# Attention outputs of a hybrid attention and gated-MLP layer: uncut fp32 probabilities and values, two branches on two halves of the array's columns

## The chip, the cores and the metric

One Trainium2 chip, one core. The metric is the device time of one execution in microseconds (us), median over runs. The kernel before takes 1041.9 us (three runs, 1041.83 to 1042.65).

## The reference, cut to what matters

One layer is computed for 1024 prompt tokens and for 8 sample tokens with cached keys. Only the prompt's attention is touched by the change. It has three branches: over compressed blocks (`o_c`), over chosen blocks (`o_s`) and over a window of 512 keys (`o_w`). Eight heads of 64 dimensions share two groups of keys and values, four heads to a group.

```python
def nsa_core(q, qpos, kc, vc, ks, vs, kw, vw, kwpos):
    ...
    s_s = jnp.einsum('bqgrd,bgqnld->bqgrnl', qg, k_sel).astype(jnp.float32) * scale
    ...
    p_s = jax.nn.softmax(s_s, axis=-1).reshape(B, Tq, N_KV, GQA, n_sel, L_SLC)
    o_s = jnp.einsum('bqgrnl,bgqnld->bqgrd', p_s.astype(dt), v_sel)
    ...
    s_w = jnp.einsum('bqgrd,bkgd->bqgrk', qg, kw).astype(jnp.float32) * scale
    p_w = jax.nn.softmax(jnp.where(m_w, s_w, NEG), axis=-1)
    o_w = jnp.einsum('bqgrk,bkgd->bqgrd', p_w.astype(dt), vw)
```

Around it stand the input projections (modulated RMS norm, then `w_in`), the rotary parts, a gated spatial MLP, a gated merge of the two branches' projections and the output projection. All inputs and outputs are fp32.

## The kernel before, in words

Most matrix products are made from halves: an fp32 value x is cut into hi (rounded to fp32r, the type of a one-pass matmul) and lo = x - hi, and a product takes three one-pass matmuls, hi by hi, hi by lo and lo by hi. Channel-major projections (`ct_proj`, line 883; tiles `mm`, weights `c0h`, `c0l`, `c1h`, `c1l`, inputs `hh`, `hl`) do that 128 channels by 344 tokens at a time. They run as "jobs" (`stream`, line 900), which fill TensorE beside decode and attention.

The order of the work on every engine is fixed when the program is built. Each piece of work is a generator that yields what it waits for. `Plan.go` (line 237) always runs a step of the stream that would wait least by the plan's own estimate of the time (`Plan.cost`, line 165, has a cost for each instruction), and the instructions go to the engines in that order. All engine calls go through a helper, so the profile shows line 217 for each of them, and tiles tell them apart. `paced` (line 871) holds the jobs back so that they last as long as the attention.

The prompt's attention works on 16 tiles (`TILES`): a group g of heads and 128 queries i. For a tile, `front` prepares the queries and the maxima. `scores` (line 1704) then walks over its spans (`spans`, line 1574): a span is a branch w (1 window, 0 chosen blocks) and 128 keys. Two fp32r matmuls give the scores of 128 keys by 512 (four heads by 128 queries) in a bank `st`, ScalarE's exponential writes `pt`, and on the diagonal GpSimd masks it. There are 132 spans in all: 60 of the window and 72 of the chosen blocks.

`low` (line 1728) cuts `pt` into halves `p`: the hi half by ScalarE or VectorE (`HI_DVE`), the lo half by VectorE or GpSimd (`ON_POOL`). `outputs` (line 1743) adds a span to the branch's bank `pv` with three one-pass matmuls. The values `vv` of a branch are kept as [v hi | 64 columns of ones | v lo], so that the first and third matmul also give the sums of p in rows 64 to 127 of the bank:

```python
pe.matmul(x, lhsT=v[:, 0:128], rhs=p2[:, 0], start=first, stop=False, skip_group_check=True)
pe.matmul(x[0:64], lhsT=v[:, 128:192], rhs=p2[:, 0], start=False, stop=False, skip_group_check=True)
pe.matmul(x, lhsT=v[:, 0:128], rhs=p2[:, 1], start=False, stop=False, skip_group_check=True)
```

`weigh` (line 1773) copies a branch's output (`u`) and its row of sums (`sr`) out of the bank, and `close` (line 1793) divides, weighs by gates and adds the branches. A matmul's place in the array follows from its operands: its weights' columns lie where the output's rows begin. In the kernel before every output begins at row 0 of its bank.

Of the kernel before, what the change touches and what calls it, by code (L numbers as in the profile page):

```python
# [24 lines left out]
EPS = 1e-6  # L25
# [3 lines left out]
class Pack:  # L29
    """Constants that depend on the shapes alone, as columns of one [128, n] array."""  # L30
# [62 lines left out]
class Plan:  # L93
    """Estimates when the engines get to what has been emitted, so that independent streams of work can be
    emitted in an order in which the engines wait little. It has no part in what is computed."""
# [35 lines left out]
    def meet(x, y):  # L131
        """Whether two accesses to a tile, as box() gives them, overlap."""
# [8 lines left out]
    def after(self, ap, writes_only, engine=None):  # L141
        """When the accesses to the elements of ap are over."""
# [22 lines left out]
    def cost(self, engine, name, outs, ins, size, start):  # L165
        if engine == "pe":
# [4 lines left out]
            elif dt == F32:  # L171
                cost, passes = max(4 * n / 2.4, 208 * m / 128), 4
# [87 lines left out]
def nsa_gmlp_step(ctx: ExitStack, tc: tile.TileContext, a: dict):  # L260
# [29 lines left out]
    def free_bank(tag):  # L290
        """Goes on when a bank can be written, as far as other streams let it."""
# [15 lines left out]
    def rows(name, n, m=128):  # L307
        """The n elements of an input on each of m partitions."""
# [38 lines left out]
    def rsqrt(out, x, scale, n, p=128):  # L347
        """out = (x * scale + EPS) ** -0.5"""
# [24 lines left out]
    def weights(todo):  # L373
        """Loads slices (key, source, columns) in order and cuts them into hi and lo, but for those used as they are."""
# [46 lines left out]
    def x_turned(first):  # L421
        """RMS-normalised x, transposed: every other tile."""
# [26 lines left out]
    def x_loads():  # L449
        """The tiles of x behind the weights of the modulation, which all wait for."""  # L450
# [38 lines left out]
    def modulation():  # L489
        """Shift and scale of the samples and the prompt (column 8), and from them h."""  # L490
# [1532 lines left out]
```

## Time and profile before

| | |
|---|---|
| median of 3 runs | 1041.9 us (1041.83 to 1042.65) |
| span of the profiled execution | 1039.6 us |
| TensorE (PE) busy | 1018.3 us, 98% of the span |
| weight loads (PEld) busy | 878.7 us, 85% |
| VectorE (DVE) busy | 657.1 us, 63% |
| ScalarE (ACT) busy | 468.5 us, 45% |
| GpSimd (POOL) busy | 305.5 us, 29% |

The profiled execution shows its span, from its first instruction to its last; no other time of it is given, and the median of the runs is 2.3 us above it. The page lists for each engine how long it was busy, in 40 slices how busy it was and which clock TensorE was granted, and for groups of instructions their number, time and what they waited for. In the name of a group `pv<-p,vv` the tile written stands left of the arrow and the tiles read stand right of it. The end of a matmul is modelled in the profile, so a matmul's cost in a stream is read from the distance of two starts in the timeline.

### The profile page before, as it was taken

To read this page: it belongs to the slowest core of one execution; us is meant where nothing else is said; L and a number is where in the kernel's file an instruction comes from. 1 tells how busy PE (TensorE), PEld (TensorE's weight loads), DVE (VectorE), ACT (ScalarE), POOL (GpSimd) and SP (SyncE) were. 2 spreads that over 40 slices of the span, in tenths; PEclk is the share of its full clock that TensorE was granted. 3 is DMA by queue.
4 is the path that set the end of the run, shared out by engine and by line. 5 is a ranking of instruction groups with operands and counts; after the bars stand their busy time and mean duration, and the time that the engine had idled before them with its cause. 6 is when DMAs were issued, how large, how long until landed. Compare 5 with 4: busy or idle time off the path is not lost. (4 is left out here: it accounts for less than half of the span.)

```text
span 1039.6 us, 16376 instructions
## 1 busy us (share of the span) xinstructions
PE 1018.3 (98%) x5747; PEld 878.7 (85%) x5747; DVE 657.1 (63%) x1372; ACT 468.5 (45%) x984; POOL 305.5 (29%) x332
## 2 busy tenths in 40 slices
PE   7999999999999999999999999999999999999998
PEld 2589977879999999987878788778788999998776
DVE  5676786354668766578787868895753147675322
ACT  5763332001332244767766677677666242232000
POOL 0453565454221110013334332433333100251000
PEclk9999999999999999999999999999999999999999
DMA  9735451103875745521212121211111478554321
GB/s 328 263 95 175 135 185 52 61 22 129 277 213 149 256 152 192 151 67 41 79 53 72 35 64 49 68 38 51 50 58 59 126 248 254 187 163 146 120 91 62
DMA packets 106311, 130.33 MB, mean 125 GB/s; under 512 B 27299, under 2 KB 71525, under 8 KB 106230
## 3 DMA queue, kind: packets, MB, share of 16 engines
q1 hardware_dynamic: 101622, 112.52, 33.7%
q0 software_dynamic: 4608, 16.78, 5.2%
q8 instruction: 45, 0.74, 0.3%
q14 instruction: 36, 0.29, 0.1%
HBM read 98.95 MB, written 30.23 MB: 124 GB/s over the span
## 5 line engine op out<-in xcount | busy, mean ns | idle before, releaser
L217 PE MATMUL pv<-p,vv 128*128 128x512 f32 (+1 forms) x396 | 111.7, 399 | 0.5 <-DVE p L217 0.4
L217 PE MATMUL mm<-hh,c0h 128*128 128x344 f32 x320 | 105.3, 329 | 0.0
L217 ACT ACTIVATE pt<-st 128x512 f32<-128x512 f32 x132 | 78.7, 596 | 58.5 <-PE st L217 56.1
L217 PE MATMUL mm<-hh,c1h 128*128 128x344 f32 x320 | 104.9, 328 | 0.0
L217 PE MATMUL mm<-hl,c0h 128*128 128x344 f32 x320 | 102.3, 320 | 0.0
L217 PE MATMUL mm<-hl,c1h 128*128 128x344 f32 x320 | 102.2, 319 | 0.0
L217 PE MATMUL mm<-hh,c1l 128*128 128x344 f32 x320 | 102.2, 319 | 0.0
L217 PE MATMUL mm<-hh,c0l 128*128 128x344 f32 x320 | 102.2, 319 | 0.0
L217 PE MATMUL st<-R,L 128*128 128x512 f32 (+1 forms) x264 | 88.2, 415 | 0.0
L217 PEld LDWEIGHTS pv<-p,vv 128*128 128x128 f32 (+1 forms) x396 | 65.7, 172 | 22.4 <-DVE p L217 1.9
L217 DVE TENSOR_TENSOR p<-pt,p 128x512 fp32r<-128x512 f32 x88 | 69.4, 794 | 17.7 <-ACT p L217 17.1
L217 POOL TENSOR_TENSOR p<-pt,p 128x512 fp32r<-128x512 f32 x44 | 60.0, 1364 | 53.9 <-ACT p L217 53.9
L217 ACT ACTIVATE p<-pt 128x512 fp32r<-128x512 f32 x94 | 59.1, 629 | 13.6 <-POOL pt L217 12.3
L217 POOL TENSOR_SCALAR_AFFINE_SELECT pt<-pt 128x512 f32<-128x512 f32 x40 | 29.3, 732 | 121.7 <-ACT pt L217 119.8
L217 PE MATMUL mx<-L,R 128*128 128x512 f32 (+3 forms) x204 | 61.7, 364 | 1.8 <-DVE bm L217 1.1
L217 PEld LDWEIGHTS mm<-hh,c1h 128*128 128x128 f32 x320 | 60.3, 188 | 2.9 <-issue 0.2
L217 PEld LDWEIGHTS mm<-hh,c0h 128*128 128x128 f32 x320 | 60.4, 189 | 2.5 <-issue 0.2
L217 PEld LDWEIGHTS mm<-hh,c1l 128*128 128x128 f32 x320 | 60.3, 188 | 2.5
L217 PEld LDWEIGHTS mm<-hh,c0l 128*128 128x128 f32 x320 | 60.3, 188 | 2.1
L217 PEld LDWEIGHTS mm<-hl,c0h 128*128 128x128 f32 x320 | 60.1, 188 | 0.0
L217 PEld LDWEIGHTS mm<-hl,c1h 128*128 128x128 f32 x320 | 60.1, 188 | 0.0
L217 ACT ACTIVATE th<-mm 128x344 f32<-128x344 f32 x68 | 30.9, 454 | 58.3 <-PE mm L217 58.0
(497 smaller groups left out, 2669.3 us busy)
## 6 DMA issues: line engine op xcount, KB each, us to landing
t_db<-th SPq DMA_DIRECT2D x24, 172.0 KB
t_da<-th SPq DMA_DIRECT2D x24, 172.0 KB
th<-t_db SPq DMA_DIRECT2D x24, 172.0 KB
th<-t_da SPq DMA_DIRECT2D x24, 172.0 KB
graw<-in_w_ada_dram SPq DMA_DIRECT2D x16, 256.0 KB
araw<-in_w_ada_dram SPq DMA_DIRECT2D x16, 256.0 KB
xt<-in_x_dram SPq DMA_DIRECT2D x8, 512.0 KB
eraw<-in_w_ada_dram SPq DMA_DIRECT2D x16, 256.0 KB
```

What stands on the lines that cost most here:

```text
L217: r = getattr(real, name)(*args, **kw)
```

## The change

The probabilities `pt` are not cut any more, nor are the values: `vv` is fp32 with 64 columns, `low` goes, and its two or three elementwise instructions of a span with it. A span has one fp32 matmul with 64 columns. The window's output goes to rows 64 to 127 of a bank and that of the chosen blocks to rows 0 to 63 of the same bank, so the two lie on different halves of the array's columns. `spans` now alternates between the branches as long as both have keys, and `outputs` emits four spans in a row.

The sums of p have no matmul of their own in a span: `total` adds the `pt` of a branch up elementwise into `acc` (VectorE, every third span GpSimd), and at the end of a tile two fp32 matmuls with 32 columns of ones, at rows 0 and 32 of a bank `mx`, sum `acc` over the keys. `weigh` reads both sums in one copy. `pt` has 8 buffers in place of 4. In `Plan.cost` an fp32 matmul with at most 64 columns counts half. The changed file has no docstrings and section comments; that part of the diff is left out here.

```diff
@@ Plan.cost
             elif dt == F32:
-                cost, passes = max(4 * n / 2.4, 208 * m / 128), 4
+                cost, passes = max(4 * n / 2.4 / (2 if m <= 64 else 1), 208 * m / 128), 4
@@ attention of the prompt
-    L1, L2, vv = ({(g, w): areg.tile(shape, FR, name=f"{n}{g}{w}") for g, w in ((0, 0), (0, 1), (1, 0))}
-                  for n, shape in (("L1", [128, T]), ("L2", [96, T]), ("vv", [128, 8, 192])))
+    L1, L2, vv = ({(g, w): areg.tile(shape, dt, name=f"{n}{g}{w}") for g, w in ((0, 0), (0, 1), (1, 0))}
+                  for n, shape, dt in (("L1", [128, T], FR), ("L2", [96, T], FR), ("vv", [128, 8, 64], F32)))
...
-    PT_BUFS, P_BUFS = 4, 4
+    PT_BUFS = 8
...
-    one = areg.tile([128, 64], F32, name="one")
+    one = areg.tile([128, 32], F32, name="one")
@@ keys
-                v = v8[:, 4 * hf:4 * hf + 4]
-                split(v[:, :, 0:64], v[:, :, 128:192], v4)
-                act.activation(v[:, :, 64:128], one[:, None, :].to_broadcast([128, 4, 64]), AF.Copy)
+                act.activation(v8[:, 4 * hf:4 * hf + 4], v4, AF.Copy)
@@ spans
-        return [(1, k) for k in range(max(0, i - 4), i + 1)] + [(0, k) for k in range(i + 1)]
+        window, chosen = [(1, k) for k in range(max(0, i - 4), i + 1)], [(0, k) for k in range(i + 1)]
+        return [x for two in zip(window, chosen) for x in two] + chosen[len(window):]
@@ scores
-                plan.add(low(g, i, n, pt), 0)
+                plan.add(total(g, i, n, w, pt), 0)
@@ low, total
-        yield lambda: flying[0] < P_BUFS
-        flying[0] += 1
-        p2 = areg.tile([128, 2, 512], FR, name="p2", bufs=P_BUFS)
-        if n % 3 in HI_DVE:
-            dve.tensor_copy(p2[:, 0], pt)
+        key = g, i, w
+        if key not in sums:
+            sums[key] = pt
         else:
-            act.activation(p2[:, 0], pt, AF.Copy)
-        yield p2[:, 0]
-        (pool if n % 3 in ON_POOL else dve).tensor_tensor(p2[:, 1], pt, p2[:, 0].bitcast(F32), op=OP.subtract)
-        waiting[0] -= 1
-        cut[g, i, n] = p2
+            old = sums[key]
+            if key not in added:
+                added.add(key)
+                sums[key] = areg.tile([128, 512], F32, name="acc", bufs=4)
+            (pool if n % 3 in ON_POOL else dve).tensor_tensor(sums[key], old, pt, op=OP.add)
+        cut[g, i, n] = pt
@@ outputs
-            o, x, todo = {}, None, spans(i)
-            for n, (w, k) in enumerate(todo):
-                yield lambda: (g, i, n) in cut and (g, w, "v") in built
-                p2 = cut.pop((g, i, n))
...
-                yield p2[:, 1]
-                v = vv[g, w][:, k, :]
-                pe.matmul(x, lhsT=v[:, 0:128], rhs=p2[:, 0], start=first, stop=False, skip_group_check=True)
-                pe.matmul(x[0:64], lhsT=v[:, 128:192], rhs=p2[:, 0], start=False, stop=False, skip_group_check=True)
-                pe.matmul(x, lhsT=v[:, 0:128], rhs=p2[:, 1], start=False, stop=False, skip_group_check=True)
...
+            todo = spans(i)
+            yield lambda: open_[0] < 2
+            open_[0] += 1
+            x = bank("pv")
+            for n0 in range(0, len(todo), 4):
+                four = range(n0, min(n0 + 4, len(todo)))
+                yield lambda: all((g, i, n) in cut for n in four) and (g, 0, "v") in built and (g, 1, "v") in built
+                pts = [cut.pop((g, i, n)) for n in four]
+                yield pts[-1]
+                for n, pt in zip(four, pts):
+                    w, k = todo[n]
+                    pe.matmul(x[64 * w:64 * w + 64], lhsT=vv[g, w][:, k, :], rhs=pt, start=n < 2, stop=False, skip_group_check=True)
+                    spanned[0] += 1
+                if four[-1] + 1 == len(todo):
+                    yield sums[g, i, 0]
+                    yield from free_bank("mx")
+                    b = bank("mx")
+                    for w in range(2):
+                        pe.matmul(b[32 * w:32 * w + 32], lhsT=one, rhs=sums.pop((g, i, w)), start=True, stop=True)
+                waiting[0] -= len(four)
                 yield 0
@@ weigh
-        act.activation(sr[64:65], x[64:65], AF.Copy)
-        if j not in s8s:
-            s8s[j] = areg.tile([128, 8], F32, name="s8", bufs=U_TILES)
-        dma(s8s[j][64 * w:64 * w + 64], sr[64:65])
+        act.activation(sr, b[0:33], AF.Copy)
+        s8s[j] = areg.tile([128, 8], F32, name="s8", bufs=U_TILES)
+        for w in range(2):
+            dma(s8s[j][64 * w:64 * w + 64], sr[32 * w:32 * w + 1])
```

TensorE's order around the outputs of two spans, before (`vv_4490` holds the values of the chosen blocks, `vv_4491` those of the window, `mm` is a job's projection, `st` the scores, `mx` the maxima):

```order
L217 MATMUL mm<-hl,c1h 128x344
L217 MATMUL st<-R,L_4485 128x512
L217 MATMUL st<-R_6627,L_4488 128x512
L217 MATMUL pv<-p_7314,vv_4491 128x512
L217 MATMUL pv<-p_7314,vv_4491 64x512
L217 MATMUL pv<-p_7314,vv_4491 128x512
L217 MATMUL mx<-kc_4495,R 128x64 x4
```

And in the changed program, where the outputs of four spans stand in a row:

```order
L217 MATMUL st<-R,L_4485 128x512
L217 MATMUL st<-R_4753,L_4488 128x512
L217 MATMUL pv<-pt,vv_4491 64x512
L217 MATMUL pv<-pt,vv_4490 64x512
L217 MATMUL pv<-pt,vv_4491 64x512
L217 MATMUL pv<-pt,vv_4490 64x512
L217 MATMUL mx<-L_4484,R 128x512
```

Three matmuls of a span became one of 64 rows, and the branches alternate. Counted over the whole program, the 164 new matmuls (132 of spans, 32 of sums) stand in 51 uninterrupted runs: 24 of four spans that alternate (window, chosen, window, chosen), 5 of one span of each branch, 14 of two sums alone, and 8 of other kinds, among them the 12 spans of the chosen blocks that have no partner in the window.

The sums of a tile on TensorE, in the changed program, between the maxima of the next tiles:

```order
L217 MATMUL mx<-L_4485,R 128x384
L217 LDWEIGHTS ident_bf
L217 MATMUL mx<-far_bf,ident_bf 128x128
L217 MATMUL mx<-acc,one 32x512 x2
L217 MATMUL mx<-L_4485,R 128x256
L217 LDWEIGHTS ident_bf
L217 MATMUL mx<-tri_bf,ident_bf 128x128
```

Both matmuls are new, 32 in the 16 tiles; the program before has nothing in their place.

TensorE's order at the start, during the modulation (`gh`, `gl`, `araw`: weights of the modulation, `xt`: rows of x that are transposed), as the difference of the two programs:

```order
 L217 MATMUL mm<-gl,cs 42x512
 L217 MATMUL mm<-araw,cT 9x512
+L217 MATMUL mx<-main,xt 128x128 x8
 L217 MATMUL mm<-gh,cs 42x512
 L217 MATMUL mm<-gl,cs 42x512
@@ -29,5 +30,4 @@
 L217 MATMUL mm<-gl,cs 42x512
 L217 MATMUL mm<-araw,cT 9x512
-L217 MATMUL mx<-main,xt 128x128 x8
 L217 MATMUL mm<-gh,cs 42x512
 L217 MATMUL mm<-gl,cs 42x512
```

Eight transposes stand a few matmuls earlier. The fp32 matmuls `mm<-araw,cT` of 9 columns are untouched, but the plan's estimate for them is halved, and the order moves in many such places up to the decode.

## Rows read from the trace of the kernel before

**Rows 1.** The page: busy time by engine; TensorE and its granted clock in 40 slices.

```profile
PE 1018.3 (98%) x5747; PEld 878.7 (85%) x5747; DVE 657.1 (63%) x1372; ACT 468.5 (45%) x984; POOL 305.5 (29%) x332
...
PE   7999999999999999999999999999999999999998
...
PEclk9999999999999999999999999999999999999999
```

**Rows 2.** Busy time by stretch: length, engines with counts, granted clock, DMA, GB/s.

```profile
0.00:36.00 36.00, 29.55 (x99) 8.85 (x100) 19.04 (x38) 19.55 (x34) 2.81 (x9) 1.00 0.95 341
36.00:150.00 114.00, 111.78 (x614) 98.85 (x613) 88.20 (x219) 57.57 (x131) 61.54 (x69) 1.00 0.48 150
150.00:260.00 110.00, 108.35 (x546) 89.25 (x544) 56.17 (x116) 14.12 (x26) 56.33 (x50) 1.00 0.22 74
455.00:805.00 350.00, 344.97 (x1945) 286.84 (x1945) 254.89 (x560) 243.65 (x516) 125.77 (x140) 1.00 0.18 55
```

**Rows 3.** Waits of TensorE from 400 to 810 us: total us, times, longest.

```profile
PE mx L217 <- DVE bm L217: 1.7, 4, 0.8
PE mx L217 <- DVE BT L217: 1.6, 2, 1.0
...
PE pv L217 <- DVE p L217: 0.4, 1, 0.4
```

**Rows 4.** TensorE's timeline around two spans: start us, length, instruction, count.

```profile
705.24 0.85 PE L217 MATMUL pv<-p,vv 128*128 128x512 f32 x3
705.93 0.32 PE L217 MATMUL mm<-hh,c0h 128*128 128x344 f32 x1
...
708.32 0.85 PE L217 MATMUL pv<-p,vv 128*128 128x512 f32 x3
709.00 0.27 PE L217 MATMUL mx<-main,pg 128*128 128x128 f32 x1
```

**Rows 5.** TensorE's timeline in the modulation: fp32 matmuls of 9 columns.

```profile
26.03 1.03 PE L217 MATMUL mm<-araw,cT 128*9 128x512 f32 x2
26.89 1.02 PE L217 MATMUL mm<-graw,cT 128*9 128x512 f32 x2
27.75 1.02 PE L217 MATMUL mm<-araw,cT 128*9 128x512 f32 x2
...
30.84 1.02 PE L217 MATMUL mm<-araw,cT 128*9 128x512 f32 x2
31.80 0.43 PE L217 MATMUL mm<-gh,cs 128*42 128x512 f32 x1
```

**Rows 6.** Timeline of the weight loads (PEld) in the same place.

```profile
26.89 0.09 PEld L217 LDWEIGHTS mm<-graw,cT 128*9 128x9 f32 x1 [0.34 <-issue]
27.32 0.09 PEld L217 LDWEIGHTS mm<-araw,cT 128*9 128x9 f32 x1 [0.34 <-issue]
```

**Rows 7.** TensorE's timeline in the decode: fp32 matmuls of 64 columns.

```profile
326.42 0.32 PE L217 MATMUL mm<-hh,c1l 128*128 128x344 f32 x1
326.58 0.32 PE L217 MATMUL mm<-hl,c1h 128*128 128x344 f32 x1
326.83 0.28 PE L217 MATMUL mx<-knT,qall 128*64 128x8 f32 x2
...
371.93 0.65 PE L217 MATMUL mx<-vcd,pcT 128*64 128x128 f32 x4
372.51 0.43 PE L217 MATMUL mx<-new,pnT 8*64 8x128 f32 x2
```

**Rows 8.** Groups of instructions: count, busy us, mean ns, idle time before them.

```profile
L217 DVE TENSOR_TENSOR p<-pt,p 128x512 fp32r<-128x512 f32 x88 | 69.4, 794 | 17.7 <-ACT p L217 17.1
L217 DVE CAST p<-pt 128x512 fp32r<-128x512 f32 x38 | 21.6, 568 | 10.2 <-ACT pt L217 10.2
L217 POOL TENSOR_TENSOR p<-pt,p 128x512 fp32r<-128x512 f32 x44 | 60.0, 1364 | 53.9 <-ACT p L217 53.9
L217 ACT ACTIVATE p<-pt 128x512 fp32r<-128x512 f32 x94 | 59.1, 629 | 13.6 <-POOL pt L217 12.3 <-PE pv L217 0.2
```

More of the change, by code (lines that the diff above doesn't have):

```diff
@@ L1486, in prepare @@
             k_load(n)
-        for n in range(PT_BUFS):
+        for n in range(4):
             e_load()
@@ L1724, in scores, with total @@
                                        base=min(sign, 0), channel_multiplier=-sign)
[L1725 removed]
+                plan.add(total(g, i, n, w, pt), 0)
             scored[0] += 1
[L1728 removed]
+    def total(g, i, n, w, pt):
         yield pt
[L1731 to L1741 removed]
+        key = g, i, w
+        if key not in sums:
+            sums[key] = pt
+        else:
+            old = sums[key]
[4 more added lines that the diff above has]
+        cut[g, i, n] = pt
@@ L1743, in outputs @@
     def outputs():
         for g, i in TILES:
-            o, x, todo = {}, None, spans(i)
-            for n, (w, k) in enumerate(todo):
-                yield lambda: (g, i, n) in cut and (g, w, "v") in built
-                p2 = cut.pop((g, i, n))
-                first = n == 0 or todo[n - 1][0] != w
-                if first:
-                    yield lambda: open_[0] < 2
-                    open_[0] += 1
-                    x = bank("pv")
-                yield p2[:, 1]
-                v = vv[g, w][:, k, :]
-                pe.matmul(x, lhsT=v[:, 0:128], rhs=p2[:, 0], start=first, stop=False, skip_group_check=True)
-                pe.matmul(x[0:64], lhsT=v[:, 128:192], rhs=p2[:, 0], start=False, stop=False, skip_group_check=True)
-                pe.matmul(x, lhsT=v[:, 0:128], rhs=p2[:, 1], start=False, stop=False, skip_group_check=True)
-                flying[0] -= 1
-                spanned[0] += 1
-                if n + 1 == len(todo) or todo[n + 1][0] != w:
-                    part.add((g, i, w))
-                    plan.add(weigh(g, i, w, x, o), 0)
+            todo = spans(i)
@@ L1765, in outputs, with weigh @@
                 yield 0
+            for w in range(2):
+                part.add((g, i, w))
+            o = {}
+            plan.add(weigh(g, i, x, b, o), 0)
             plan.add(close(g, i, pgTs.pop((g, i)), o), 0)
     ON_POOL = (1,)
-    HI_DVE = (2,)
-    pgTs, cut = {}, {}
-    waiting, flying, scored, open_ = [0], [0], [0], [0]
-    def weigh(g, i, w, x, o):
+    pgTs, cut, sums, added = {}, {}, {}, set()
+    waiting, scored, open_ = [0], [0], [0]
+    def weigh(g, i, x, b, o):
         j = TILES.index((g, i))
+        yield b
+        sr = areg.tile([33, 512], F32, name="sr", bufs=2)
+        act.activation(sr, b[0:33], AF.Copy)
+        s8s[j] = areg.tile([128, 8], F32, name="s8", bufs=U_TILES)
+        for w in range(2):
+            dma(s8s[j][64 * w:64 * w + 64], sr[32 * w:32 * w + 1])
@@ L1776, in weigh @@
         yield x
         yield lambda: tiles[1] > j - U_TILES
-        u = areg.tile([128, 2, 128], F32, name="u", bufs=2 * U_TILES)
-        sr = areg.tile([65, 512], F32, name="sr", bufs=2)
-        act.activation(sr[64:65], x[64:65], AF.Copy)
-        if j not in s8s:
-            s8s[j] = areg.tile([128, 8], F32, name="s8", bufs=U_TILES)
-        dma(s8s[j][64 * w:64 * w + 64], sr[64:65])
-        x = x.rearrange("p (c a q) -> p c a q", c=2, a=2)
-        for par in range(2):
-            act.activation(u[64 * par:64 * par + 64], x[0:64, :, par, :], AF.Copy)
+        us = [areg.tile([128, 2, 128], F32, name="u", bufs=2 * U_TILES) for _ in range(2)]
@@ L1787, in weigh @@
+        for w, u in enumerate(us):
+            xw = x[64 * w:64 * w + 64].rearrange("p (c a q) -> p c a q", c=2, a=2)
+            for par in range(2):
+                act.activation(u[64 * par:64 * par + 64], xw[:, :, par, :], AF.Copy)
         open_[0] -= 1
-        o[w] = u
+        o.update(enumerate(us))
     U_TILES, s8s = 2, {}
```

1 line of the change is left out of this document (removed).

## The prediction

> **What bounds the kernel now.** I read the page first: TensorE is busy for 1018.3 of 1039.6 us, 98%, and its granted clock stays at the full 2.4 GHz from the first slice to the last [rows 1]. No other engine is over 63%. The stretches say the same of the place that is changed: from 455 to 805 us TensorE is busy for 345.0 of 350.0 us, with VectorE at 254.9, ScalarE at 243.7 and GpSimd at 125.8 [rows 2]. What TensorE waits for there comes to a few us: 1.7 for `bm`, 1.6 for `BT`, and 0.4, once, for a half of p [rows 3]. So the kernel lasts as long as TensorE's stream of matmuls does. A matmul that TensorE is spared is a gain in full, and work taken from the other engines can give back no more than those waits. The reader should count the time that the stream loses and gains, start to start.
>
> **What the outputs cost before.** Three one-pass matmuls of 512 columns take 705.93 - 705.24 = 0.69 and 709.00 - 708.32 = 0.68 us [rows 4]. With a little for spans at less favourable neighbours I take 0.70, edges between kinds of matmul included. 132 spans times 0.70 is **92.4 us**. The sums of p are in it; they cost nothing of their own.
>
> **What an fp32 matmul costs.** The modulation has uncut fp32 matmuls with 9 columns, and two facts of them carry the sum. First, one call is two records: rows of "x2" start at 26.03, 26.89 and 27.75, 0.86 us apart, so a record takes **0.43 us**, twice a one-pass matmul's 512 / 2.4 = 0.213 [rows 5]. Second, the records follow each other with a weight load of their own each, 0.43 apart (26.89, 27.32) [rows 6]. Having few columns makes nothing cheaper: with 64 columns, four records a fourth as long take 372.51 - 371.93 = 0.58, 0.145 each with edges, against 0.43 / 4 = 0.108 [rows 7]. An fp32 matmul of the change is thus two records of 0.43, and 164 of them (132 spans, 32 sums) are 328 records. Laid end to end they are 328 x 0.43 = 141.0 us.
>
> **What the halves of the array save.** This is the open price. Every matmul of the kernel before writes from row 0 of its bank, so no two neighbours have separate columns and the trace has no pair to read. The bounds: nothing is saved (141.0), or a pair takes the time of one. The runs, counted in records, give the second bound. A run of four alternating spans is 4 records long (24 runs: 96), a pair 2 (5: 10), two sums 2 (14: 28), the other eight kinds 42 together. That is 176 x 0.43 = 75.7 us.
>
> Between the two I choose by the order of the records. A window span W is W1, W2, a chosen span C is C1, C2, and TensorE gets W1, W2, C1, C2. If it starts them in that order, W2 must wait for W1's columns, and C1 stands behind W2. So C1 runs beside W2, the next W1 beside C2, and only the first and last record of a run are alone. A run of n alternating matmuls then takes n + 1 record lengths, not n: four spans 5 (24: 120), a pair 3 (5: 15), two sums 3 (14: 42), the others 51. The sum is 228 x 0.43 = **98.0 us**. I take this because the two records one after the other are in rows 5 and 6, and starts in program order are what every stretch of the timeline that I read shows.
>
> The Trainium skill, "TensorE: Matmul & The Clock Gate", section "Part 3: Packing small matmuls — row/col tiling", says that matmuls start and end strictly in program order while those on different tiles overlap. No run here shows such an overlap yet; applied to two records a matmul it gives the same 98.0.
>
> **Edges.** A change between a one-pass matmul over all columns and an fp32 one over some costs time on both sides. On the way in 326.83 - 326.58 = 0.25 in place of 326.58 - 326.42 = 0.16, so 0.09 [rows 7]; on the way out 31.80 - 30.84 = 0.96 in place of 0.86, so 0.10 [rows 5]. 51 runs times 0.2 is **10.2 us**. If half of the edge is hidden it is 5, if all of it nothing.
>
> **The other engines.** VectorE loses 88 subtractions and 38 casts (69.4 + 21.6 us) and gets 72 additions of the same size (72 x 0.794 = 57); GpSimd has 28 additions (28 x 1.364 = 38) for 44 subtractions (60.0); ScalarE loses 94 copies (59.1) [rows 8]. TensorE's 98% covers all of that, before and after, so I cost it at nothing. If the lighter VectorE removes the waits of rows 3, at most 3.7 us come back. Additions stand on GpSimd's queue between masks of `pt`, which the exponential's users wait for, but GpSimd has 224 free us of 350 [rows 2]. The copies of the sums and the sums' DMAs on SP's queue are as many bytes as before and off the path. I also put nothing on the single bank of a tile and on the deeper `pt`.
>
> **The start.** The plan's estimate for the 16 uncut fp32 matmuls of the modulation is halved, though they lie alone on their columns and will take 0.86 as before. So the order is moved up to the decode by an estimate that is 16 x 0.43 = 7 us too short. The first 36 us are set by the loads (DMA at 0.95), and TensorE idles only 2.2 us from 36 to 150 and 1.7 from 150 to 260 [rows 2]. I put 0 on it, with a gain of at most 3.9 and a loss as large.
>
> **The sum.** 98.0 + 10.2 - 92.4 = **+15.8 us**. Against the profiled span that is 1039.6 + 15.8 = 1055.4; the median stands 2.3 above the span, so **1057.7 us**. Its own range is 1047 to 1062: with edges at half, the waits gone and a gain at the start it is 1045, but hardly all of these at once; a loss of 4 at the start is the upper end.
>
> **Rivals.**
> - *Full overlap: faster.* C1 starts with W1, although W2 stands before it, and a pair takes one matmul's time. Place: the same 51 runs. Price: 75.7 + 10.2 - 92.4 = -6.5, so 1035.4, and with the waits of rows 3 gone 1031.7. It decides as soon as the outputs and their edges stay under 92.4 us, that is under 82.2 of records. For it: separate columns need not wait for each other, and weight loads are shown to run beside matmuls [rows 6]. Against it: nothing in the timeline starts ahead of a matmul that was issued earlier. The Trainium skill's section named above gives starts about 4 ns apart for matmuls on different tiles, and a gain of 2.38 for three column tiles; that is this rival if two records count as one, and no run here shows it.
> - *No overlap: the change does not do what it says.* The halves run one after the other: 141.0 + 10.2 - 92.4 = +58.8, so 1100.7. For it: no row shows two matmuls streaming at once.
> - *The sums are late.* At the end of each of 16 tiles TensorE stands before the sums until the last addition is done, 0.79 us on VectorE or 1.36 on GpSimd [rows 8]. At most 16 x 1.36 = 22 us on top of the forecast, 1079. Against it: in 14 of 16 tiles other matmuls stand between the last span and the sums, and VectorE gets lighter.
>
> **How the numbers follow.** Forecast 0.48; full overlap 0.33; no overlap 0.10; late sums or another wait 0.09. A measurement of this kernel can tell 0.2%, about 2.1 us. Full overlap gives a gain of 6.5 to 10.2 us; 0.31 of its 0.33 count as faster and the rest as the same, for edges dearer than 0.2; some of the forecast's tail, with hidden edges, adds 0.03 to faster and 0.05 to the same. Faster 0.34, same 0.07, slower 0.59. The two likeliest cases have different signs, so the range goes from full overlap, 1031, to a forecast with a bad start, 1064, and leaves out the 0.10 of no overlap and most of the 0.09. The forecast alone would be 1047 to 1062.
>
> **What would show it.** Right: in the timeline of the changed kernel four alternating spans take about 5 x 0.43 = 2.15 us plus edges from their first start to the next full matmul, the first record of a C starts together with the second record of the W before it, 0.43 after that W began, and two sums take about 1.3. Full overlap shows as 1.7 for four spans, no overlap as 3.4. TensorE stays at 98% and at 2.4 GHz. Late sums would show as waits of `mx` for `acc`. The forecast is wrong if the outputs take under 92 us together, or if the time outside them moves by more than 4 us.

## The result, and the profile after

The changed kernel takes **1069.7 us** (median of four runs, 1067.25 to 1070.98) against 1041.9 (1040.96 to 1042.65) for the kernel before beside it: a ratio of 1.0269, 95% interval 1.0254 to 1.0285, slower by 27.8 us. The forecast was +15.8. The direction was right; the time lies outside the range of 1031 to 1064, and the steps behind the forecast were not the ones that cost.

The page of the changed kernel, its busy times and slices, answers to [rows 1]:

```profile
PE 1029.7 (96%) x5679; PEld 835.6 (78%) x5679; DVE 615.2 (58%) x1310; ACT 399.4 (37%) x866; POOL 284.6 (27%) x316
...
PE   7999999999999999999989999999999969999998
...
PEclk9999999999999999999999999999999979999999
```

Every other engine has less to do, as costed. But TensorE falls from 98% to 96%, and in one slice, near 870 us, its activity and clock both dip. The stretches, with the columns of [rows 2] and the two stretches after the attention added:

```profile
0.00:36.00 36.00, 29.68 (x97) 9.85 (x98) 20.16 (x40) 20.42 (x36) 5.64 (x11) 0.95 0.94 321
36.00:150.00 114.00, 110.02 (x597) 95.27 (x595) 81.58 (x205) 56.87 (x129) 57.61 (x65) 1.00 0.50 153
150.00:260.00 110.00, 109.62 (x545) 89.95 (x544) 58.45 (x126) 13.93 (x25) 57.36 (x50) 1.00 0.20 66
455.00:805.00 350.00, 341.11 (x1873) 243.41 (x1871) 210.83 (x497) 166.72 (x383) 91.15 (x111) 0.98 0.19 55
...
835.00:930.00 95.00, 85.01 (x514) 81.49 (x513) 42.51 (x86) 27.04 (x54) 7.74 (x10) 0.93 0.64 199
930.00:1067.00 137.00, 132.20 (x641) 110.61 (x639) 61.90 (x100) 19.03 (x27) 21.38 (x21) 1.00 0.36 117
```

The stretch from 835 to 930 us, of which [rows 2] say nothing, reads so in the kernel before:

```profile
835.00:930.00 95.00, 94.83 (x601) 94.16 (x601) 60.44 (x113) 29.64 (x51) 18.12 (x16) 1.00 0.70 219
```

Two things are new: ten us without a matmul in 835 to 930, and a mean clock of 0.98 and 0.93 where it was 1.00. In the slower stretches the granted clock is the lower of the two levels, 1.2 GHz: 13.6 us in three pieces of the attention (from 478.7, 553.8 and 598.2 us), 13.6 us from 864.4, and 3.4 us from 17.9. Work done at half the clock takes twice as long, so half of the time that TensorE works in such a stretch is lost. Time in which it waits there is lost to the wait and not to the clock, and from 864.4 us it works for 5.55 us only, so 2.8 are lost:

```profile
864.40:878.00 13.60, 5.55 (x18) 4.74 (x18) 3.99 (x9) 3.93 (x9) 0.00 (x0) 0.50 0.70 225
```

What TensorE waits for, over the whole kernel (total us, times, longest; [rows 3] are the same view of the attention alone):

```profile
PE st L217 <- ACT xh L217: 8.6, 3, 6.0
PE mx L217 <- DVE wm L217: 6.9, 6, 2.3
...
PE mx L217 <- DVE ce L217: 1.6, 1, 1.6
...
PE mx L217 <- DVE bm L217: 1.2, 3, 0.5
```

In the kernel before TensorE waits 0.2 us for `wm` (the window's maxima) and nothing for `xh` (the hi half of the gated merge's input). All its waits of over 1 us in the attention stand at the new sums of p. The sums take a bank `mx`, of which the program has two, and the maxima need the same banks. The rows of TensorE, and of ScalarE, which copies the sums out (`sr`):

```profile
475.29 1.05 PE L217 MATMUL mx<-acc,one 128*32 128x512 f32 x4 [0.30 <-DVE wm L217]
...
479.09 0.69 PE L217 MATMUL mx<-L,R 128*128 128x384 f32 x1 [2.11 <-DVE wm L217]
...
481.80 0.58 ACT L217 ACTIVATE sr<-mx 33x512 f32<-33x512 f32 x1
...
554.15 1.92 PE L217 MATMUL mx<-pt,one 128*32 128x512 f32 x4 [2.30 <-DVE wm L217]
...
593.92 1.05 PE L217 MATMUL mx<-acc,one 128*32 128x512 f32 x4 [0.42 <-DVE bm L217]
...
597.17 0.41 PE L217 MATMUL mx<-L,R 128*128 128x384 f32 x1 [1.63 <-DVE ce L217]
...
598.86 0.58 ACT L217 ACTIVATE sr<-mx 33x512 f32<-33x512 f32 x1
```

In the wait of 2.30 us the sums stand before a bank that VectorE has not yet read. In those of 2.11 and 1.63 us the sums of 475.29 and 593.92 still hold their bank, as they are copied out at 481.80 and 598.86 only, and the maxima behind them have to do with the other one. The three pieces at half clock begin in these waits or at most 1 us behind them. No run gave the sums a bank of their own, so this is read from the timeline and not tested.

Following four matmuls through both timelines says where the 27.8 us lie:

| starts at, us | before | after | later by |
|---|---|---|---|
| first job matmul | 235.77 | 240.46 | 4.7 |
| last job matmul | 846.77 | 860.39 | 13.6 |
| first merge matmul (`xh`) | 846.93 | 861.77 | 14.8 |
| last matmul of that stage (`xl`) | 938.13 | 965.93 | 27.8 |
| end of the span | 1039.6 | 1067.4 | 27.8 |

So **4.7 us** come up to the first job, **8.9** from the first to the last job, with the decode and the attention, and **14.2** behind them, in the merge, which the change does not touch. Each part can be divided into TensorE's idle time, half of its working time at the lower clock, and the rest, which is what the matmuls themselves take at the full clock:

| part | later by | more idle time | lost at half clock | rest |
|---|---|---|---|---|
| up to the first job matmul | 4.7 | 1.6 | 1.7 | 1.4 |
| first to last job matmul | 8.9 | 4.5 | 6.4 | -2.0 |
| last job to last merge matmul | 14.2 | 10.3 | 2.8 | 1.1 |

The matmuls of the attention and its jobs thus gain 2.0 us; idle time and the clock cost more than that.

The outputs themselves are faster than forecast. TensorE's timeline around a tile's two sums and a run of four spans, with the columns of [rows 4]:

```profile
707.17 0.32 PE L217 MATMUL mm<-hl,c1h 128*128 128x344 f32 x1
707.42 1.05 PE L217 MATMUL mx<-acc,one 128*32 128x512 f32 x4
708.41 0.72 PE L217 MATMUL st<-R,L 128*128 128x512 f32 x2
...
709.17 1.94 PE L217 MATMUL pv<-pt,vv 128*64 128x512 f32 x8
711.04 0.51 PE L217 MATMUL st<-R,L 128*128 128x512 f32 x1
```

Its weight loads in that run (PEld):

```profile
709.17 0.20 PEld L217 LDWEIGHTS pv<-pt,vv 128*64 128x64 f32 x4 [0.29 <-issue]
709.66 0.14 PEld L217 LDWEIGHTS pv<-pt,vv 128*64 128x64 f32 x2 [0.29 <-issue]
710.09 0.14 PEld L217 LDWEIGHTS pv<-pt,vv 128*64 128x64 f32 x2 [0.28 <-issue]
```

From first start to the next full matmul the four spans take 711.04 - 709.17 = 1.87 us. The prediction gave 2.15 for a staggered order and 1.7 for full overlap, plus edges. The eight records start 0, 7, 481, 488, 910, 917, 1340 and 1346 ns after the first: always two together. The trace does not name the half that a record writes; that the two are one of each half follows from experiment 1, where no two records on one half start together. Two sums take 708.41 - 707.42 = 0.99, with their way out, where 1.3 was forecast.

The additions on VectorE and GpSimd, to hold against [rows 8] (count, busy us, mean ns, idle time before them):

```profile
L217 POOL TENSOR_TENSOR acc<-acc,pt 128x512 f32<-128x512 f32 x28 | 36.0, 1286 | 87.9 <-ACT pt L217 79.1
...
L217 DVE TENSOR_TENSOR acc<-acc,pt 128x512 f32<-128x512 f32 x44 | 33.1, 755 | 30.2 <-ACT pt L217 18.4
```

### The profile page after: what moved, and what is told of

Read it like the earlier page. It is cut to its first block, busy times and chain, and to the rows that moved or that the text cites. A ratio compares the mean times of both kernels' runs of the same rounds, so it can differ in the third digit from the quotient of the medians.

```text
span 1067.4 us, 15998 instructions
## 1 busy us (share of the span) xinstructions
PE 1029.7 (96%) x5679; PEld 835.6 (78%) x5679; DVE 615.2 (58%) x1310; ACT 399.4 (37%) x866; POOL 284.6 (27%) x316
## 4 chain that ended last, share of the span: by engine, by line
PE 84%; DVE 5%; DMA 4%; issue 2%; ACT 2%; SPq 1%; POOL 1%; DVEq 0%; ACTq 0%; POOLq 0%
PE mm L217 35%; PE pv L217 20%; PE mx L217 15%; PE st L217 14%; DMA araw<-in_w_ada_dram 1%; SPq L217 1%; DMA gk<-in_cache_k_slc_dram,idx 1%; DMA zt<-z_db 1%; DVE wm L217 0%; POOL m L217 0%; DVE gl L217 0%; DMA gk<-in_cache_k_cmp_dram,idx 0%; DVE ce L217 0%; DVE bm L217 0%; DMA oraw<-in_w_out_dram 0%
## 5 line engine op out<-in xcount | busy, mean ns | idle before, releaser
L217 PE MATMUL mm<-hh,c0h 128*128 128x344 f32 x328 | 108.6, 331 | 0.0
L217 PE MATMUL mm<-hh,c0l 128*128 128x344 f32 x328 | 104.7, 319 | 0.0
L217 PE MATMUL st<-R,L 128*128 128x512 f32 (+1 forms) x264 | 91.1, 427 | 0.0
L217 PE MATMUL pv<-pt,vv 128*64 128x512 f32 x264 | 73.4, 634 | 0.0
L217 DVE TENSOR_REDUCE bm<-mx 128x8 f32<-128x512 f32 x72 | 47.8, 686 | 23.6 <-PE mx L217 23.3
L217 POOL TENSOR_TENSOR acc<-acc,pt 128x512 f32<-128x512 f32 x28 | 36.0, 1286 | 87.9 <-ACT pt L217 79.1
L217 PEld LDWEIGHTS st<-R,L 128*128 128x128 f32 (+1 forms) x264 | 43.5, 196 | 11.8 <-issue 8.2
L217 PEld LDWEIGHTS mx<-L,R 128*128 128x128 f32 x204 | 39.1, 196 | 15.8 <-DVE wm L217 5.7
L217 DVE TENSOR_REDUCE wm<-mx 128x4 f32<-128x512 f32 x60 | 39.9, 685 | 19.0 <-PE mx L217 18.5
L217 DVE TENSOR_TENSOR acc<-acc,pt 128x512 f32<-128x512 f32 x44 | 33.1, 755 | 30.2 <-ACT pt L217 18.4
```

Of the source, the lines that this page charges most:

```text
L217: r = getattr(real, name)(*args, **kw)
```

## The experiments

Theory after the result: the halves overlap in full and the outputs gain, and what was lost lies outside them, at the start and at the merge. The rivals: the outputs are the loss after all; the additions on VectorE and GpSimd are.

**1. Do the halves overlap?** In e3_one_half the instructions stay in their order, but both branches are put on the same columns (the line of `weigh` that reads the bank follows and is left out here; the outputs of the two branches are mixed up).

```diff
-                    pe.matmul(x[64 * w:64 * w + 64], lhsT=vv[g, w][:, k, :], rhs=pt, start=n < 2, stop=False, skip_group_check=True)
+                    pe.matmul(x[0:64], lhsT=vv[g, w][:, k, :], rhs=pt, start=n < 2, stop=False, skip_group_check=True)
```

> The changed kernel, same order of instructions, but both branches write to rows 0 to 63 of the bank, so they share one half of the columns (the outputs of the two branches are then mixed up). Theory (in the changed kernel a pair of branches takes the time of one): the 60 pairs lose their overlap, 60 x 0.86 = 51.6 us at full clock, 1069.7 + 52 = 1121, 1112 to 1126; in the timeline four spans take 3.4 us. Rival (the halves overlap only by a record, as forecast): 24 x 3 + 5 x 1 + 14 records less, 1069.7 + 39 = 1109 or less. Rival (no overlap in the changed kernel at all): 1070.

Measured 1118.97 us, ratio 1.0751 (1.0726 to 1.0775), 49 us above the changed kernel. The timeline of a run of four spans in it:

```profile
694.42 3.65 PE L217 MATMUL pv<-pt,vv 128*64 128x512 f32 x8
698.00 0.50 PE L217 MATMUL st<-R,L 128*128 128x512 f32 x1
```

The run takes 698.00 - 694.42 = 3.58 us against 1.87: eight records of 0.43 one after the other, and the way out. From the first maxima to the last job, without idle time and half clock, the matmuls take 459.8 us against 408.3 in the changed kernel: 51.5 more, and 60 pairs of 0.86 are 51.6. The overlap is shown, and so is its worth.

**2. Does the order within a run matter?** e4_wwcc puts the spans in the order W W C C (a second line of the edit, which moves the `start` flag to each branch's first span, is left out here).

```diff
-        return [x for two in zip(window, chosen) for x in two] + chosen[len(window):]
+        n = len(window) // 2 * 2
+        out = [x for j in range(0, n, 2) for x in window[j:j + 2] + chosen[j:j + 2]]
+        return out + [x for two in zip(window[n:], chosen[n:]) for x in two] + chosen[len(window):]
```

> The changed kernel with the four spans of a run in the order window, window, chosen, chosen in place of window, chosen, window, chosen. In the changed kernel the first records of a window span and of the chosen span behind it start 7 ns apart, although the window's second record was thought to stand between them. Theory (each half of the columns takes its own matmuls as soon as its columns are free): four spans still take 1.87 us and the kernel 1067 to 1073. Rival (only two neighbouring matmuls on different halves run together): only the two in the middle overlap, four spans take 3 x 0.86 + edges = 2.75 us, 24 runs lose 0.86 each, about 1090, 1082 to 1094.

Measured 1077.14 us, ratio 1.0340 (1.0319 to 1.0361). The kernel is 7 us slower than the changed one, but not by the run, in its timeline:

```profile
699.79 1.94 PE L217 MATMUL pv<-pt,vv 128*64 128x512 f32 x8
701.66 0.50 PE L217 MATMUL st<-R,L 128*128 128x512 f32 x1
```

701.66 - 699.79 = 1.87 us again. The first two records of the run start 14 ns apart (12 to 14 over the runs of this kind); the second can only be C's, although a whole W stands between it and the first. Of the 7 us 5 lie in the merge: its last `xl` is 35.3 us later than in the kernel before and its last job 15.8, so the merge loses 19.5 us where the changed kernel loses 14.2.

**3. The start.** b1_plan_line is the kernel before with nothing but the changed line of the plan; e1_plan_9 is the changed kernel with the halving kept to the matmuls that do lie beside another.

```diff
-                cost, passes = max(4 * n / 2.4, 208 * m / 128), 4
+                cost, passes = max(4 * n / 2.4 / (2 if m <= 64 else 1), 208 * m / 128), 4
```

> The kernel before with one line of the change: the plan's estimate of fp32 matmuls with at most 64 columns halved. Up to the attention its order of instructions is that of the changed kernel, and the outputs are those of before. Theory (the plan's line costs time at the start): the changed kernel reached its first job 4.7 us later than the kernel before (240.5 against 235.8), so this one takes 1041.9 + 4.7 = 1046.6, 1045 to 1049, with a stretch of half clock near 18 us. Rival (the line is harmless, the delay at the start comes from elsewhere or is chance of one profile): 1041 to 1043.

```diff
-                cost, passes = max(4 * n / 2.4 / (2 if m <= 64 else 1), 208 * m / 128), 4
+                cost, passes = max(4 * n / 2.4 / (2 if m in (32, 64) else 1), 208 * m / 128), 4
```

> The changed kernel with the halved estimate for 32 and 64 columns alone, so that the 9-column matmuls of the modulation keep their full estimate. Up to the attention its order is that of the kernel before. Theory: the 4.9 us that the changed kernel was behind at the first maxima are back, and the rest stays: 1069.7 - 4.9 = 1064.8, 1062 to 1068. Rival (the delays later take up whatever is gained at the start, because the end is set by a chain in the attention): 1069 to 1071.

b1 took 1045.72 us, ratio 1.0047 (1.0032 to 1.0061): 5.2 us for an estimate, with no other line changed. Its stretch from 36 to 150 us has fewer matmuls than [rows 2] show for the same time:

```profile
36.00:150.00 114.00, 109.91 (x590) 95.56 (x588) 80.42 (x204) 56.27 (x128) 55.69 (x65) 0.99 0.48 149
```

590 in place of 614; its first job matmul starts at 242.01 us, against 235.77. e1 took 1058.99, ratio 1.0173 (1.0156 to 1.0190), with the first job back at 236.19. It gained 10.7, twice what was expected: of the attention's 13.6 us at half clock 3.4 are left (from 475.5 us). That these go with the start was not foreseen, and why they do is not shown. In e1 the last job stands 2.3 us later than in the kernel before and the last `xl` 17.5, so most of what is left of the loss is the merge's.

**4. The merge.** Its input is loaded by SyncE's queue. In the changed kernel the queue's rows read (start, length, transfer, count):

```profile
846.36 6.04 SPq L217 DMA_DIRECT2D o_d<-u  x4
853.93 1.27 SPq L217 DMA_DIRECT2D zt<-z_db  x3
855.24 0.90 SPq L217 DMA_DIRECT2D t_da<-th  x2
```

And in the kernel before:

```profile
823.10 0.80 SPq L217 DMA_DIRECT2D o_d<-u  x2
826.31 1.27 SPq L217 DMA_DIRECT2D zt<-z_db  x3
```

The first loads of `zt` start at 853.93, behind the attention's last outputs, 6.5 us ahead of the last job; before, they start at 826.31, also behind the last outputs, but 20.5 us ahead of the last job. What follows on TensorE, the merge's matmuls with the idle time before each:

```profile
861.77 0.42 PE L217 MATMUL st<-xh,c0h 128*128 128x344 f32 x1 [1.06 <-ACT c0h L217]
...
863.66 0.42 PE L217 MATMUL st<-xh,c0h 128*128 128x344 f32 x1 [0.57 <-ACT xh L217]
...
870.76 0.66 PE L217 MATMUL st<-xh,c0h 128*128 128x344 f32 x1 [6.04 <-ACT xh L217]
...
873.99 0.65 PE L217 MATMUL st<-xh,c0h 128*128 128x344 f32 x1 [2.01 <-ACT xh L217]
...
875.02 0.49 PE L217 MATMUL pv<-xh,c0h 128*128 128x344 f32 x1
875.30 0.49 PE L217 MATMUL pv<-xh,c0l 128*128 128x344 f32 x1
```

The work that used to cover these loads is gone: after the last output 258 job matmuls were left before the change, 144 are left now (counted in the two orders). At 0.16 us each that is 18 us less cover. 144 is no chance number: `paced` keeps 6 pieces of 24 matmuls for the time after the attention (`PACE_REST`), so in the changed kernel the jobs ran ahead as far as they are let, and before they did not. The waits come to 10.3 us more idle time, and the clock falls with them: matmuls of 344 columns stand 0.28 us apart (875.02, 875.30) where they stand 0.16 apart at 2.4 GHz. Of the 13.6 us at half clock 8.0 are the waits themselves, so 2.8 are lost. 10.3 + 2.8 = 13.1 of the 14.2; the other 1.1 shows no wait. Two ways to cover the loads were tried. The first is to hold more jobs back: e2_rest11 does so, and e6_plan_rest9 does less of it on top of e1.

```diff
-    SPANS, PACE_LEAD, PACE_FRONT, PACE_REST = 132, 12, 14, 6
+    SPANS, PACE_LEAD, PACE_FRONT, PACE_REST = 132, 12, 14, 11
```

> The changed kernel with the jobs held back further: 11 pieces of 24 matmuls are kept for after the attention in place of 6 (PACE_REST). Theory (the merge starts without cover because the jobs were used up inside the attention; 144 of their matmuls were left after the last output, 258 before): the 9.4 us of waiting and the 13.7 us of half clock between the jobs' end and the merge's end go, about 9.4 + 6.8 = 16 at most, and TensorE has 5 x 24 x 0.157 = 18.8 us of jobs less to fill the attention with. If the attention has enough other work, 1069.7 - 14 = 1055.7, 1053 to 1060. Rival (the attention is a chain of its own that the jobs only fill up): the time taken from the end comes back as waiting in the attention, 1066 to 1074.

> The changed kernel with the full estimate for the 9-column matmuls and 9 pieces of the jobs kept for after the attention in place of 6: 216 of their matmuls stand behind the last output, 144 before the edit, 258 in the kernel before. Theory (the uncovered start of the merge costs 9.9 us of waits and 13.7 us of half clock, together about 16, and 72 matmuls of 0.157 cover 11 us of it): 1059.0 - 8 = 1051, 1047 to 1055. Rival (as with 11 pieces and the changed plan, what the end gains the attention or the loads of the jobs' weights lose): 1056 to 1061.

e2 took 1067.70 us, ratio 1.0265 (1.0243 to 1.0286). The waits for `xh` are gone, and from the first `xh` to the last `xl` it takes 91.5 us (before 91.2, after 104.2). Yet the last job starts 26.4 us later than before: from the first maxima to the last job TensorE idles 19.2 us in place of the changed kernel's 9.8, and 5.7 of them are a new wait for the weights `c0h`:

```profile
PE mx L217 <- ACT c0h L217: 5.7, 1, 5.7
```

e6 (9 in place of 11) took 1061.79, ratio 1.0201 (1.0184 to 1.0218), 2.8 more than e1. Jobs are a fixed sum; holding them back moves the hole.

The other way is to load earlier. f3_plan_zt6 is e1 with the merge's first products (branch `b`) loaded five chunks ahead in place of two; g1_before_zt6 makes the same edit in the kernel before.

```diff
-        tiles_ = []
-        for n in range(len(todo) + 2):
+        tiles_, A = [], 5 if br == "b" else 2
+        for n in range(len(todo) + A):
...
-                tiles_.append([late["mr"].tile([128, 344], F32, name=x, bufs=3)[:, :m] for x in ("zt", "zx")[:1 + (br == "a")]])
+                tiles_.append([late["mr"].tile([128, 344], F32, name=x, bufs=6 if x == "zt" else 3)[:, :m] for x in ("zt", "zx")[:1 + (br == "a")]])
...
```

> The changed kernel with the full estimate for the 9-column matmuls and the first products of the merge loaded five ahead in place of two (six buffers of zt in place of three); the attention's order is as it was with the estimate alone. Theory (after the jobs' end TensorE waits 9.9 us for xh, whose loads stand in a row behind each other on SP's queue, and its clock falls to half for 13.7 us): the waits for xh fall to under 4 us, 1059.0 - 10 = 1049, 1046 to 1053. Rival (the merge waits for the attention's last gated sum, which opens its memory, so earlier loads cannot start): 1057 to 1060.

> The kernel before, with the merge's products loaded five chunks ahead instead of two (6 buffers of zt). Theory: the loads are late only where attention ends late against the jobs; in the kernel before 258 job matmuls lie after the last output and cover them, so the edit gives nothing: 1041.7 (1040.5 to 1043). Rival: the merge is slowed by its loads in any order, and the 6 us that the same edit gave the changed kernel are a gain that has nothing to do with the change: 1035 to 1038.

f3 took 1053.00 us, ratio 1.0115 (1.0097 to 1.0133), 6.0 less than e1. TensorE's waits in it from 830 to 900 us:

```profile
PE st L217 <- ACT c0h L217: 2.6, 1, 2.6
PE st L217 <- ACT xh L217: 0.8, 1, 0.8
```

In e1 `xh` cost 9.0. What stays is the next one in line, the weights, and a clock of 0.51 from 851 to 861 us. g1 took 1041.38, ratio 0.9997 (0.9987 to 1.0007): in the kernel before the edit is worth nothing. So the hole is owed to the order in which the attention ends, not to the merge's loads as such.

**5. The additions.** e5_no_adds leaves 72 of the 100 out, f2_plan_no_adds does so on top of e1, and g3_plan_zt6_no_adds on top of f3.

```diff
-            (pool if n % 3 in ON_POOL else dve).tensor_tensor(sums[key], old, pt, op=OP.add)
+            if n < 4:
+                (pool if n % 3 in ON_POOL else dve).tensor_tensor(sums[key], old, pt, op=OP.add)
```

> The changed kernel without 72 of the 100 additions of p (those from the fifth span of a tile on, so the sums and the outputs divided by them are not the reference's). Theory (the additions stand on VectorE's queue before the reductions of the maxima, so TensorE waits for wm, bm and ce, 9.7 us in the changed kernel, and its clock falls to half after the longest waits, 13.7 us in the attention): most of these waits and of the half clock go, 1069.7 - 9 = 1061, 1057 to 1065. Rival (TensorE's waits come from the order, in which the attention has too little ready work): the waits for wm and bm stay within 2 us and the time within 3 us of 1069.7.

> The changed kernel with the full estimate for the 9-column matmuls and without 72 of the 100 additions of p (sums and the outputs divided by them are not the reference's). Theory (start, additions and merge are separate costs; the 15.2 us of the run without additions add to the start's): 1069.7 - 10.7 - 12 = 1047, 1043 to 1050. Rival (both edits remove the same waits): 1053 to 1056.

> The changed kernel with the plan's halving kept to 32 and 64 columns, the merge's products loaded five ahead, and 72 of the 100 additions of p left out (the sums of p are incomplete, and with them the outputs' divisor). Theory: without the additions the merge is covered already, so this stays where the same kernel without early loads was: 1050.8 (1049 to 1052.5). Rival: the two gains, 8 and 6 us, are independent: 1044.5 to 1047.

e5 took 1054.52 us, ratio 1.0126 (1.0109 to 1.0143), 15.2 less than the changed kernel; f2 1050.76, ratio 1.0086 (1.0069 to 1.0102), 8.2 less than e1; g3 1049.76, ratio 1.0093 (1.0067 to 1.0119), where f2 was. So leaving additions out and loading early do not add up: they close the same hole. Without additions the attention ends earlier against the jobs, 168 job matmuls are left and the waits for `xh` are gone; in their place a wait of 3.3 us for the weights `c1l` came up ahead of the last job:

```profile
PE pv L217 <- DVE c1l L217: 3.3, 1, 3.3
```

The matmuls themselves take the same time (408.4 us from the first maxima to the last job, 408.3 in the changed kernel, without idle time and half clock). VectorE was at 58%, so it seems that the additions cost through the order and the chain of a tile and not through its busy time; that is argued from these rows and not shown apart.

Then all of them should go to GpSimd, which has most room. f1_plan_pool is that edit on top of e1.

```diff
-    ON_POOL = (1,)
+    ON_POOL = (0, 1, 2)
```

> The changed kernel with the full estimate for the 9-column matmuls and all 100 additions of p on GpSimd (100 x 1.29 = 129 us of the 390 us of the attention). Theory (VectorE's queue is what the attention waits for: without 72 of the additions the changed kernel was 15 us faster): VectorE loses 72 x 0.755 = 54 us, TensorE's waits for wm, bm and ce shrink, and 1059.0 goes to 1050, 1046 to 1055. Rival (GpSimd is slower for each addition and stands between the masks of p, so the outputs wait for GpSimd instead, or the order alone made the difference): 1057 to 1066.

It took 1070.93, ratio 1.0283 (1.0266 to 1.0300), 12 **more** than e1: the theory was wrong. TensorE's waits for `wm` fell from 6.4 to 1.8, but those for `bm` are 4.9, and new ones for GpSimd's masks (`pt`) came up; 17 us at half the clock, 10 of them idle, lie about the merge's waits:

```profile
PE mx L217 <- DVE bm L217: 4.9, 6, 2.6
...
PE pv L217 <- POOL pt L217: 1.4, 2, 1.0
```

Moving the additions moves the late operand; an idle engine at 1.30 us an addition is no relief where the next step stands behind it.

**6. Shorter runs.** e7_plan_pairs is e1 with outputs in groups of two spans, f4_plan_pairs_pool adds the edit of f1, g2_plan_pairs_zt6 the early loads.

```diff
-            for n0 in range(0, len(todo), 4):
-                four = range(n0, min(n0 + 4, len(todo)))
+            for n0 in range(0, len(todo), 2):
+                four = range(n0, min(n0 + 2, len(todo)))
```

> The changed kernel with the full estimate for the 9-column matmuls and outputs emitted by two spans in place of four: 77 runs in place of 51, 198 of the jobs' matmuls behind the last output. Theory (groups of four make the attention wait for four exponentials and both branches' values, so it falls behind and the jobs run out): the attention is done earlier against the jobs, the uncovered start of the merge shrinks by 54 x 0.157 = 8.5 us, and 26 more runs cost 26 x 0.2 = 5: 1059.0 - 3 = 1056, 1052 to 1059. Rival (the size of the groups is not what holds the attention up, only the edges count): 1059 + 5 = 1064, 1061 to 1066.

> The changed kernel with the full estimate for the 9-column matmuls, outputs emitted by two spans, and all additions of p on GpSimd; 144 of the jobs' matmuls behind the last output. Theory (VectorE's queue holds the attention up): 1056.6 - 6 = 1050, 1046 to 1054, if the start of the merge stays covered, and 10 more if it does not. Rival (GpSimd's additions hold the outputs up instead): 1060 to 1068.

> The changed kernel with the plan's halving kept to 32 and 64 columns, outputs in groups of two instead of four, and the merge's products loaded five ahead. Theory: in groups of two attention ends earlier against the jobs (198 job matmuls left) and the merge is covered already, so the early loads add nothing: 1056.6 (1055 to 1058). Rival: the gains of both edits add up, since the merge has a delay of its own: 1050 to 1052.

e7 took 1056.58 us, ratio 1.0146 (1.0118 to 1.0175); g2 1058.98, ratio 1.0164 (1.0142 to 1.0187); f4 1067.78, ratio 1.0249 (1.0228 to 1.0270). In g2 the two stretches read:

```profile
455.00:805.00 350.00, 341.50 (x1814) 231.44 (x1814) 206.59 (x487) 164.85 (x377) 92.07 (x111) 0.98 0.18 54
835.00:930.00 95.00, 95.00 (x608) 95.00 (x608) 51.05 (x100) 29.34 (x57) 11.60 (x14) 1.00 0.71 220
```

The merge runs as before the change, at 95.00 of 95.00 us and full clock, with 198 jobs left to cover it. But 77 runs in place of 51 fill the attention with edges: its last job starts 17.7 us later than before. e7 gives the price of an edge. Its matmuls from the first maxima to the last job are those of e1, in 26 more runs; without idle time and half clock they take 418.8 us against 408.7, so a run costs 10.1 / 26 = 0.39 us beyond its records. Early loads add nothing to pairs, as the theory of the hole had it.

No version of the uncut outputs came below the kernel before. The best that computes everything is f3, 1053.0.

## Why the prediction was wrong

- **"If it starts them in that order, W2 must wait for W1's columns, and C1 stands behind W2."** This step failed. Each half of the columns takes its own records as it comes free; first records start 7 ns apart (and 14 ns in e4, past a whole matmul of the other half). The price of 98.0 for the records should have been the 75.7 of full overlap, which was the first rival: 22.3 us too much in this term. The Trainium skill's "TensorE: Matmul & The Clock Gate", section "Part 3: Packing small matmuls — row/col tiling", gives about 4 ns between starts on different tiles; the 7 ns here are near it. Its strict program order, taken record by record as the prediction did, does not hold in these rows.
- **"51 runs times 0.2 is 10.2 us."** Mis-sized. f3 shows the attention at full clock but for 3.4 us, and all its matmuls can be set against those of the kernel before, start to start, from the first maxima to the last job, idle time and half clock taken out. Outputs and sums: 94.7 us before (92.4 in the prediction), 83.1 in f3, of which 75.7 are records; so 7.4 us are ways out, 0.15 a run. Scores, which mostly stand ahead of a run: 67.3 to 72.1. Jobs and small matmuls around the runs: 5.2 more together, six more job matmuls not counted. The edges thus cost 7.4 + 4.8 + 5.2 = 17.4 us, 0.34 a run, in place of 0.2; that this growth is edge is borne out by e7, where each further run costs 0.39. 75.7 + 17.4 - 94.7 = -1.6: the change of method is a draw, neither the forecast's +15.8 nor the rival's -6.5.
- **"I put 0 on it, with a gain of at most 3.9 and a loss as large"** (the start). Wrong place and size: 4.7 us in the milestones, 5.2 in b1, just above the bound. The prediction named the cause, an estimate 7 us too short, and then costed the wait it could see in the stretches and not the order that such an estimate makes.
- **"TensorE's 98% covers all of that, before and after, so I cost it at nothing."** Failed in two ways. What TensorE waits for in the attention rises (6.9 us for `wm`), by 4.5 us in all, and the clock halves for 13.6 us, at a loss of 6.4; less the 2.0 that the matmuls gain this is the 8.9 of the milestones. And the stage behind was not looked at: the cover of the merge's loads, 14.2 us, half of the result. The prediction said that the time outside the outputs would move by no more than 4 us; even with every edge counted to the outputs it moved by some 29, the whole 27.8 and the 1.6 gained. Its other sign of being wrong came true as well: the outputs and sums take under 92 us, 83.1.
- **The late sums** did not come as described: TensorE's waits name `wm`, `ce` and `bm`, not `acc`. The sums are late in another way: they wait for a bank `mx`, or the maxima behind them do, 0.30 + 2.11 + 2.30 + 0.42 + 1.63 = 6.8 us in the rows above, a wait that the prediction did not have. The additions matter (e5, f2), by where they put the end of the attention.
- **What held:** the size of a record (0.43), the count of records and runs, that the halves overlap, that other engines get lighter. That the sign came out right is luck: the outputs and their edges, which were to cost 15.8 us, gain 1.6, and the loss is made of terms that were put at nothing, 4.7 + 8.9 + 14.2 = 27.8.

Why the attention of the changed kernel ends later against its jobs was narrowed, not settled: the additions are part of it (168 jobs left without most of them), the groups of four another (198 in pairs), and neither reaches the 258 of before. Where 144 are left, the jobs were held at the bound of `paced`; what made the planner take so many of them was not tested. The half-clock stretches in the attention were not taken away alone either; most of them went with the start's order in e1.

## What to carry to other kernels

When every instruction's order comes from a planner, an edit of a cost is an edit of the whole program: one line cost 5 us in stages that the change does not touch, so compare the order stage by stage to the end, and ask of each stage what covers its first loads. Where TensorE is nearly always busy, a wait of a few us can be dearer than its length, since the clock may halve beside it; here waits of 1.6 to 2.3 us in the attention went with 1.5 to 3.2 us lost at half clock. A small matmul that borrows a bank from another step can make that step wait. Small-column matmuls are cheapest in long runs with a partner (here even that was a draw), and every change between them and full ones must be priced on both sides.

## What the runs showed of the hardware

Two fp32 matmuls on different halves of the columns run wholly side by side: four spans take 1.87 us on two halves and 3.58 on one. The partner need not be the next instruction: in W W C C the two halves still start 14 ns apart and the run takes the same 1.87. A record without a partner costs the full 0.43 us, and the way out of a run some 0.13 to 0.15 more (0.99 for two sums, 1.01 for a pair). With what the matmuls about it lose, a further run costs 0.39 us (e7 against e1). Around an idle time of 2.3 us (up to 554.15, waiting for `wm`) and those of 6.0 and 2.0 us in the merge the granted clock was at its lower level for 3.4 and 13.6 us, which cost 1.5 and 2.8 us on top of the waits; in the kernel before its mean is 1.00 in every slice and stretch shown.
